# Two feed-forward blocks of a hybrid transformer: shared products in two alternating sets of four PSUM banks, and one weight sum moved to an accumulating transfer

## The chip, the cores and the metric

The kernel runs on one core of one Trainium2 chip. The metric is device time in microseconds (us) of one execution, as the median of the runs. A core has TensorE (PE, matmuls, with a sequencer for weight loads), VectorE (DVE), ScalarE (ACT), GpSimd (POOL), SyncE (SP, which here only issues transfers) and 16 DMA engines between HBM and the on-chip memory SBUF. Matmuls write to PSUM, used here as eight banks of 128 x 512 float32 values.

## The reference

Two layers over 256 tokens of width 2048, in float32. Each adds a mixer (gated delta rule and a linear recurrence in the first layer, two kinds of attention in the second) and then a feed-forward block of inner width 5632; a last norm follows.

```python
def swiglu(hn, w_gate, w_up, w_down):
    return (jax.nn.silu(hn @ w_gate) * (hn @ w_up)) @ w_down

for layer in range(DEPTH):
    h = h + mixer(rmsnorm(h, ...), ...)
    h = h + swiglu(rmsnorm(h, ffn_norm[layer]), ffn_w_gate[layer], ffn_w_up[layer], ffn_w_down[layer])
return rmsnorm(h, final_norm)
```

The change touches the two feed-forward blocks alone.

## The kernel before, in words

**Precision.** Every float32 operand is split into a high half (rounded to the matmul's type, by a cast on ScalarE) and a low half (the rest, by a subtraction on VectorE). A product is the sum of three matmuls: high by high, high by low, low by high. `X` and `hid` hold the split activations, 128 x 128 pieces of which are the stationary operand; the weights stream past as 128 x 512.

**Blocks.** `ffn` (from line 659) goes through 17 blocks per layer: 11 gate/up blocks of 512 inner columns and 6 down blocks, in three pieces of (4 gate/up + 2 down), (4 + 2), (3 + 2). A block has four output banks `F[t, i]`: token half `t` by column half `i` (gate or up; or the two 512-wide halves of the outputs). The weights of a block come as tiles of 128 x 1024 float32 (512 KB), one per step.

**Plain steps and sevens.** A plain step is one weight tile against both token halves: 12 matmuls. A "seven" takes a 2 x 2 arrangement of four weight tiles (b11, b12, b21, b22) and 2 x 2 activation blocks, and forms their product from seven products instead of eight, with sums of weight tiles and sums of activation tiles (`comb`, made by `combine`). A seven is seven steps of 6 matmuls. Most gate/up blocks have two sevens and 8 plain steps; the first block of a layer has none; the last down blocks have one.

Before, `steps` gives each block four banks `F` in the PSUM pool `acc` and four banks `M` for the shared products in the pool `msp`. At the block's end `ends` (from line 427) copies M0 out on ScalarE and makes the three sums on VectorE into a tile `e` of SBUF; `values` adds them to `F` (L721), applies scale and SiLU on ScalarE (L722) and multiplies gate and up (L727); `residual` adds `h` and `F` (L741, L746). `turned` transposes the result on TensorE (`Ph`, L673) and splits it into `hid`. The three weight sums of a seven are made on VectorE in a tile `T` (L485, L492), a fourth by an accumulating transfer from GpSimd's queue (L487).

**Order.** `stream` walks the list of steps and readies them four ahead: `load` (SP's queue, L175), the cast (L547), the low half (L560). From the second block of a layer on, TensorE, VectorE and ScalarE run in the order written; in the first block a scheduler orders them.

**Memory.** The pools `wr` (three raw tiles), `wh` and `wl` (high and low halves) live through the whole program. The pools `og`/`hid`, `fp` and `mx` are closed and opened anew for every mixer and every feed-forward stage (`phase`). `load` sets its count to -12 at a phase's start, so that the first twelve raw tiles of a stage come from `wr`; after that four of seven come from four buffers `raw4` in `mx`. High halves of two steps in six (`thi`) and low halves of two in five (`tlo`) lie in `fp`.

**The seam.** A stage is entered behind the mixer's output projection, whose last group `g` = 3 ends with the sums into `h` (L361), the squares of `h` for the norm (`sumsq`, L319, into a scratch tile `junk`), the transposes `Pt` (L328) and the split into `X` (L329, L330).

Of the kernel before, what the change touches and what calls it, by code (L numbers as in the profile page):

```python
# [11 lines left out]
T = 256  # L12
# [35 lines left out]
def body(tc, A, out):  # L48
# [266 lines left out]
    def sumsq(g, *ts):  # L315
        for t in ts or range(2):
            j = (mx.tile([128, 1024], F32, name="junk", tag="T", bufs=2)[:, 0:512] if more else
                 mx.tile([128, 512], F32, name="junk", tag="t2", bufs=4))
            S.activation(j, h[:, t, g * 512:(g + 1) * 512], AF.Square, accum_out=ssp[:, t, g:g + 1])  # L319
# [69 lines left out]
    def combine(f, r=None):  # L389

        c = mx.tile([128, 4, 2, 128], F32, name="cc4", tag="T", bufs=2)
# [12 lines left out]
    def combine_x(x4, r=None):  # L404

        f = mx.tile([128, 4, T], F32, name="cf", tag="T", bufs=2)
        V.tensor_tensor(out=f, in0=x4[:, :, 0].bitcast(F32), in1=x4[:, :, 1].bitcast(F32), op=ALU.add)
        return run(combine([f[:, :, t * 128:(t + 1) * 128] for t in range(2)], r))
# [29 lines left out]
    class Step:  # L438


        def __init__(self, high, use, unit=None):
            self.high, self.use, self.unit = high, use, unit

    def steps(src, x, comb, nd, early, late):

        ns = len(comb)
        plain = [(i, u) for m in range(nd) if m not in comb for u in (2 * m, 2 * m + 1) for i in range(2)]
        n, F, M = len(plain) // 2, {}, {}

        def bank(t, i):  # L450
            if (t, i) not in F:
                F[t, i] = Bank(acc.tile([128, 512], F32, name=f"F{t}{i}", tag="acc"), n + (ns if t * i == 0 else 0))
            return F[t, i]

        def bank7(j):
            if j not in M:
                M[j] = Bank(ms([128, 512], f"M{j}"), ns)
            return M[j]

        def xs(k, t):  # L460
            return [x(k)[:, j, t * 128:(t + 1) * 128] for j in range(2)]

        def high(i, u, b, name):
            def f():
                b[name] = load(src(i, u))
                return b[name]
            return f

        def simple(i, u):
            b = {}  # L470

            def use(w, tt=(0, 1)):
                for t in tt:
                    bank(t, i).add(lambda kk: xs(2 * u + kk, t), w)
            return Step(high(i, u, b, "b"), use, (i, use))

        def seven(m):
            b = {}
            cx = lambda i: lambda kk: [comb[m]()[:, j, i, kk] for j in range(2)]
            q = lambda j, t: lambda kk: xs(4 * m + 2 * j + kk, t)  # L480

            def first():
                load_b12()
                b["t"] = mx.tile([128, 1024], F32, name="T", tag="T", bufs=2)
                V.tensor_tensor(out=b["t"], in0=b["b11"], in1=b["b12"], op=ALU.add)  # L485

                G.dma_start(b["b12"], src(1, 2 * m + 1), accum_op=ALU.add)  # L487
                return b["t"]

            def more_of(name):  # L490
                def f():
                    V.tensor_tensor(out=b["t"], in0=b["t"], in1=b[name], op=ALU.add)  # L492
                    return b["t"]
                return f

            load_b12 = high(1, 2 * m, b, "b12")
            return [Step(high(0, 2 * m, b, "b11"), lambda w: bank7(0).add(q(0, 0), w)),
                    Step(first, lambda w: bank7(1).add(cx(0), w)),
                    Step(high(1, 2 * m + 1, b, "b22"), lambda w: bank(0, 1).add(cx(3), w)),
                    Step(more_of("b22"), lambda w: bank7(2).add(cx(2), w)),  # L500
                    Step(high(0, 2 * m + 1, b, "b21"), lambda w: bank(0, 0).add(q(1, 0), w)),
                    Step(more_of("b21"), lambda w: bank(1, 0).add(q(1, 1), w)),
                    Step(lambda: b["b12"], lambda w: bank7(3).add(cx(1), w))]

        sevens = [y for m in comb for y in seven(m)]
        plain = [simple(*y) for y in plain]
        if not sevens:
            return plain, F, M
        mid = len(plain) - early - late
        order = plain[:early]  # L510
        for g in range(mid + 1):
            order += sevens[g * len(sevens) // (mid + 1):(g + 1) * len(sevens) // (mid + 1)]
            order += plain[early + g:early + g + 1] if g < mid else plain[early + mid:]
        return order, F, M
# [16 lines left out]
    def stream(acts, guard):  # L531
# [4 lines left out]
        ready = [y for y in acts if isinstance(y, Step)]  # L536
        at = [0, 0]
        g = None

        def ahead(n):  # L540

            while at[0] < min(n + 1, len(ready)):
                y, k = ready[at[0]], at[0]
                y.raw = y.high()
# [6 lines left out]
            while at[1] < min(n, len(ready)):  # L551
                low(at[1])

        def low(k):
            if k < at[1]:
                return
            y = ready[k]
            y.lo = (fp.tile([128, 1024], F32R, name="tlo", tag="tlo", bufs=2) if k % 5 in (1, 3) else
                    wl.tile([128, 1024], F32R, name="wlo"))
            V.tensor_sub(y.lo, y.raw, y.hi.bitcast(F32))  # L560
            at[1] = k + 1

        n = 0
        for y in acts:
            if isinstance(y, Step):
                if y is guard[0]:
                    g = tc.manual_schedule(engines={V.engine, S.engine, PE.engine})
                    g.__enter__()
                ahead(n + 1 + 3)
                y.use((y.hi, y.lo))  # L570
                if y.unit:
                    tick()
                n += 1
            else:
                y()
# [81 lines left out]
    def ffn(L, then, fin=None):  # L657

        gu, dn = A[f"gu{L}"], A[f"dn{L}"]
        cx, ch, acts, guard, left = {}, {}, [], [None], []  # L660
        todo = {}

        def turned(hid, j, want, soon):
# [3 lines left out]
            def first():  # L667
                a = todo.pop(j)
                o["P"] = []
                for t in range(2):  # L670
                    P = ms([128, 4, 128], "Ph")
                    for i in range(4):
                        PE.transpose(P[:, i], a[:, 2 * t, i * 128:(i + 1) * 128], tb["ident"])  # L673
# [3 lines left out]
                if want:  # L677

                    o["f"] = [a[:, 2 * t + 1].rearrange("p (k n) -> p k n", n=128) for t in range(2)]
# [15 lines left out]


            put = {2: first, 3: second}
            if want:
                put.update({8: part, 14: part, **({19: last} if soon else {})})
            return put, [last] if want and not soon else []  # L700

        def spread(order, put):

            for n, y in enumerate(order):
                acts.extend(put.get(n, []))
                acts.append(y)

        def values(hid, j, F, M, ns):

            o = {}  # L710
            rs = lambda t: nrm["rs"][:, t:t + 1]

            def bank_sums():
                o["a"] = ends(M) if ns else sums()

            def half(i):
                def f():
                    for t in range(2):
                        v = o["a"][:, 2 * t + i]
                        if ns:  # L720
                            V.tensor_tensor(out=v, in0=F[t, i].t, in1=v, op=ALU.add)  # L721
                        S.activation(v, v if ns else F[t, i].t, AF.Copy if i else AF.Silu, scale=rs(t))  # L722
                return f

            def product():
                a = o["a"]
                V.tensor_tensor(out=a[:, 0::2], in0=a[:, 1::2], in1=a[:, 0::2], op=ALU.mult)  # L727
                todo[j] = a

            return bank_sums, half(0), half(1), product  # L730

        def residual(p, F, M):

            o = {}

            def bank_sums():
                o["e"] = ends(M)
                left[:] = [o["e"]]
                for t in range(2):
                    et = o["e"][:, 2 * t:2 * t + 2].rearrange("p a n -> p (a n)")  # L740
                    V.tensor_tensor(out=et, in0=h[:, t, 1024 * p:1024 * (p + 1)], in1=et, op=ALU.add)  # L741

            def half(i):
                def f():
                    for t in range(2):
                        V.tensor_tensor(out=h[:, t, (2 * p + i) * 512:(2 * p + i + 1) * 512], in0=F[t, i].t,  # L746
                                        in1=o["e"][:, 2 * t + i], op=ALU.add)
                return f

            return bank_sums, half(0), half(1)  # L750

        b, late, turn, rest, next_rest = 0, None, None, [], []
# [811 lines left out]
```

## Time and profile before

| | |
|---|---|
| Median of 3 runs | 2218.5 us (2218.19 to 2218.76) |
| Span of the profiled execution | 2217.3 us |
| TensorE busy | 2200.4 us (99%) |
| VectorE busy | 1961.3 us (88%) |
| ScalarE busy | 1333.7 us (60%) |
| Feed-forward stages in the trace | about 430 to 1125 us, and 1518 to 2208 us |
| Loads of the feed-forward weights | 352 + 176 from SP, 40 + 20 accumulating from GpSimd, 512 KB each |

The span runs from the first to the last instruction in the trace. Busy time of an engine is the union of its instructions; a matmul is drawn to the end of its pipeline, so neighbouring matmuls overlap in the drawing. In the lists of instructions the columns are start, length, engine, line, operation, output<-inputs, shapes; what stands in brackets is the idle time before it and the instruction that ended it. Groups give busy time, mean of one in ns, and idle time before.

### The profile page before, as it was taken

The numbers are of one execution on the slowest core, as the hardware profiler recorded it, in microseconds if no ns is written. First come the engines' busy times: TensorE is split into PE (matmuls) and PEld (weight loads), VectorE is DVE, ScalarE is ACT, GpSimd is POOL, SyncE is SP. The second block draws the span as 40 slices with busy tenths as digits, with TensorE's granted clock in tenths as the row PEclk, the third lists the DMA queues.
The fourth block names the chain that finished last, engine by engine and source line by source line (L and its number), as shares of the span: only waits on it lengthen the run. The fifth ranks groups of instructions, "written<-read, shape, count | busy, mean of one in ns | idle before, by whom it ended". The sixth has DMA issues, their size and how long they took to land.

```text
span 2217.3 us, 30619 instructions
## 1 busy us (share of the span) xinstructions
PE 2200.4 (99%) x10960; PEld 1840.2 (83%) x10960; DVE 1961.3 (88%) x2664; ACT 1333.7 (60%) x1787; POOL 54.0 (2%) x66
## 2 busy tenths in 40 slices
PE   9999999999999999999999999999999999999998
PEld 8888888888888888888888888888888888888886
DVE  8899676679999999999996688857899999999998
ACT  6786664556655666466664554545666566655665
POOL 0000000000000000000000000000000000000000
PEclk9999999999999999999999999999999999999999
DMA  7545446667777778677664565556678777777784
GB/s 284 158 145 167 136 151 188 204 210 222 235 226 247 211 215 246 214 229 235 195 201 154 154 188 171 162 181 218 204 214 237 232 224 222 237 224 233 232 243 138
DMA packets 126569, 453.79 MB, mean 205 GB/s; under 512 B 14128, under 2 KB 15664, under 8 KB 126288
## 3 DMA queue, kind: packets, MB, share of 16 engines
q1 hardware_dynamic: 117488, 420.10, 58.2%
q0 software_dynamic: 8640, 31.46, 8.5%
q8 instruction: 86, 1.41, 0.3%
q14 instruction: 67, 0.55, 0.1%
q10 hardware_dynamic: 288, 0.27, 0.0%
HBM read 449.68 MB, written 2.10 MB: 204 GB/s over the span
## 4 chain that ended last, share of the span: by engine, by line
PE 88%; DVE 8%; issue 2%; DMA 1%; ACT 1%; DVEq 0%; ACTq 0%; POOLq 0%; SPq 0%
PE F L420 14%; PE F L419 14%; PE F L421 14%; PE Pw L201 11%; PE Pw L206 6%; PE M L421 5%; PE M L419 5%; PE M L420 5%; PE Px L305 3%; PE Px L307 3%; PE Px L306 3%; DVE wlo L560 1%; PE Ph L673 1%; DVE e L721 1%; DVE tlo L560 1%
## 5 line engine op out<-in xcount | busy, mean ns | idle before, releaser
L181 ACT CAST whi<-raw 128x1024 fp32r<-128x1024 f32 x245 | 256.8, 1051 | 261.7 <-PE Pw L201 85.3
L547 ACT CAST whi<-raw 128x1024 fp32r<-128x1024 f32 x362 | 372.0, 1048 | 51.1 <-PE F L421 31.1
L182 DVE TENSOR_TENSOR wlo<-raw,whi 128x1024 fp32r<-128x1024 f32 x245 | 299.0, 1222 | 114.7 <-PE Pw L206 37.2
L201 PE MATMUL Pw<-X,whi 128*128 128x512 f32 x1088 | 388.3, 400 | 0.0
L206 PE MATMUL Pw<-X,wlo 128*128 128x256 f32 x1088 | 304.6, 280 | 0.2
L419 PE MATMUL F<-whi,X 128*128 128x512 f32 x698 | 273.1, 391 | 0.6 <-DVE h L746 0.6
L421 PE MATMUL F<-whi,X 128*128 128x512 f32 x698 | 272.1, 390 | 0.0
L560 DVE TENSOR_TENSOR wlo<-raw,whi 128x1024 fp32r<-128x1024 f32 x214 | 260.6, 1220 | 9.2 <-ACT whi L547 5.3
L420 PE MATMUL F<-wlo,X 128*128 128x512 f32 x650 | 253.2, 390 | 0.0
L201 PEld LDWEIGHTS Pw<-X,whi 128*128 128x128 f32 x1088 | 204.2, 188 | 47.2 <-issue 0.5
L547 ACT CAST whi<-T 128x1024 fp32r<-128x1024 f32 x110 | 116.1, 1055 | 197.2 <-DVE T L492 119.1
L206 PEld LDWEIGHTS Pw<-X,wlo 128*128 128x128 f32 x1088 | 205.3, 189 | 1.6 <-DVE wlo L182 0.7
L560 DVE TENSOR_TENSOR tlo<-raw,whi 128x1024 fp32r<-128x1024 f32 x148 | 180.6, 1220 | 7.9 <-ACT whi L547 6.0
L547 ACT CAST thi<-raw 128x1024 fp32r<-128x1024 f32 x166 | 173.5, 1047 | 13.6 <-PE F L421 8.7
L419 PEld LDWEIGHTS F<-whi,X 128*128 128x128 f32 x698 | 131.1, 188 | 27.7 <-issue 1.1
L421 PEld LDWEIGHTS F<-whi,X 128*128 128x128 f32 x698 | 131.0, 188 | 27.3
L547 ACT CAST thi<-T 128x1024 fp32r<-128x1024 f32 x70 | 74.0, 1057 | 130.9 <-DVE T L485 61.9
L492 DVE TENSOR_TENSOR T<-T,raw 128x1024 f32<-128x1024 f32 x120 | 146.7, 1223 | 1.7
L420 PE MATMUL F<-tlo,X 128*128 128x512 f32 x370 | 144.1, 389 | 0.3 <-DVE tlo L379 0.3
L420 PEld LDWEIGHTS F<-wlo,X 128*128 128x128 f32 x650 | 122.1, 188 | 24.9
L560 DVE TENSOR_TENSOR wlo<-raw,thi 128x1024 fp32r<-128x1024 f32 x102 | 124.5, 1221 | 8.5 <-PE F L420 4.4
L419 PE MATMUL F<-whi,hid 128*128 128x512 f32 x336 | 131.3, 391 | 0.0
(445 smaller groups left out, 4691.1 us busy)
## 6 DMA issues: line engine op xcount, KB each, us to landing
raw<-in_gu SPq DMA_DIRECT2D x352, 512.0 KB, 4.6
raw<-in_dn SPq DMA_DIRECT2D x176, 512.0 KB, 4.7
raw<-in_w0w SPq DMA_DIRECT2D x72, 512.0 KB, 3.7
raw<-in_wo SPq DMA_DIRECT2D x64, 512.0 KB, 3.6
raw<-in_w1w SPq DMA_DIRECT2D x64, 512.0 KB, 3.6
raw<-in_gu POOLq DMA_DIRECT2D x40, 512.0 KB, 7.8
raw<-in_w1x SPq DMA_DIRECT2D x32, 512.0 KB, 3.7
raw<-in_dn POOLq DMA_DIRECT2D x20, 512.0 KB, 7.3
```

The lines of the kernel that those rows point to most:

```text
L181: S.copy(hi, raw)
L182: V.tensor_sub(lo, raw, hi.bitcast(F32))
L201: PE.matmul(P.rearrange("p a b -> p (a b)"), hi[:, kk], X[:, k].rearrange("p a b -> p (a b)"), start=k == 0, stop=False)
L206: PE.matmul(P[:, 0], lo[:, kk], X[:, k, 0], start=False, stop=k == NK - 1)
L305: PE.matmul(Ps[t], x[:, 0, ts], hi[:, kk], start=k == 0, stop=False)
L306: PE.matmul(Ps[t], x[:, 0, ts], lo[:, kk], start=False, stop=False)
L419: PE.matmul(self.t, xh, hi[:, kk], start=self.i == kk == 0, stop=False)
L420: PE.matmul(self.t, xh, lo[:, kk], start=False, stop=False)
L421: PE.matmul(self.t, xl, hi[:, kk], start=False, stop=kk == 1 and self.i == self.n - 1)
L492: V.tensor_tensor(out=b["t"], in0=b["t"], in1=b[name], op=ALU.add)
L547: S.copy(y.hi, y.raw)
L560: V.tensor_sub(y.lo, y.raw, y.hi.bitcast(F32))
```

## The change

- A class `Mix` takes the place of `steps`, `Bank` and the `M` banks. The shared products go into the block's own four banks: M0 into F00, the second into F01, the third into F11, the fourth into F10. Between steps `middle` turns these into the output sums, in PSUM: a copy of F00 to SBUF (ScalarE), two sums (VectorE), a copy back to F01 (ScalarE), two more sums (VectorE). Then the remaining products of the sevens and the plain steps are added on top.
- Blocks use the pools `acc` and `msp` in turn. The last four plain steps of a block are placed between the first products of the next.
- `values` and `residual` read the banks directly.
- Of the three weight sums of a seven, two stay on VectorE, in place in the tile of b11; the third (adding b21) is a second accumulating transfer from GpSimd.
- Raw tiles have tags: `ha`, `hb`, `hc` (two buffers each in `mx`) for b11, b12, b22, and `raw` for the others, five buffers of which three are in `wr` and two in `mx`. Loads are asked for up to eight steps ahead. In the first block of a layer the first ten steps take turns over `raw`, `ha`, `raw`, `hb`, `raw`, `hc`.
- Scratch tiles `T` and `e` go; `a` and `de` (one buffer each) come. `hid` is one tile for the whole stage. GpSimd's descriptor area in SBUF is set to 8192 bytes.

```diff
-            j = (mx.tile([128, 1024], F32, name="junk", tag="T", bufs=2)[:, 0:512] if more else
+            j = (mx.tile([128, 1024], F32, name="junk", tag="a", bufs=1)[:, 0:512] if more else
...
+    class Mix:
...
+            sevens = [self.seven(m) for m in comb]
+            self.early = [y[i] for i in range(4) for y in sevens]
+            self.direct = [y[i] for i in range(4, 7) for y in sevens]
...
+        def simple(self, i, u, first):
...
+            k = 2 * u + i
+            return Step(("raw", "ha", "raw", "hb", "raw", "hc")[k % 6] if first and k < 10 else "raw",
+                        lambda raw: nc.sync.dma_start(raw, self.src(i, u)), use, unit=(i, use))
...
+            def first_sum():
+                V.tensor_tensor(out=b["b11"], in0=b["b11"], in1=b["b12"], op=ALU.add)
                 G.dma_start(b["b12"], src(1, 2 * m + 1), accum_op=ALU.add)
...
+            def second_sum():
+                V.tensor_tensor(out=b["b11"], in0=b["b11"], in1=b["b22"], op=ALU.add)
+                return b["b11"]
+
+            def third_sum():
+                G.dma_start(b["b11"], src(0, 2 * m + 1), accum_op=ALU.add)
+
+            y = [Step("ha", get("b11", 0, 2 * m), lambda w: self.add(0, 0, q(0, 0), w)),
+                 Step("hb", get("b12", 1, 2 * m), lambda w: self.add(0, 1, cx(0), w), first_sum),
+                 Step("hc", get("b22", 1, 2 * m + 1), lambda w: self.add(1, 1, cx(2), w), second_sum, third_sum),
+                 Step(None, None, lambda w: self.add(1, 0, cx(1), w), lambda: b["b12"]),
+                 Step(None, None, lambda w: self.add(0, 1, cx(3), w), lambda: b["b22"]),
+                 Step("raw", get("b21", 0, 2 * m + 1), lambda w: self.add(0, 0, q(1, 0), w)),
+                 Step(None, None, lambda w: self.add(1, 0, q(1, 1), w), lambda: b["b11"])]
...
+        def middle(self):
...
+            def copy():
+                o["d"] = mx.tile([128, 2, 512], F32, name="de", tag="de", bufs=1)
+                S.copy(o["d"][:, 0], F[0, 0])
+
+            def sums():
+                d, e = (o["d"][:, j] for j in range(2))
+                V.tensor_tensor(out=d, in0=F[1, 1], in1=d, op=ALU.add)
+                V.tensor_tensor(out=e, in0=F[0, 1], in1=d, op=ALU.subtract)
+
+            def back():
+                S.copy(F[0, 1], o["d"][:, 1])
+
+            def last():
+                d, e = (o["d"][:, j] for j in range(2))
+                V.tensor_tensor(out=F[1, 1], in0=e, in1=F[1, 0], op=ALU.subtract)
+                V.tensor_tensor(out=F[1, 0], in0=F[1, 0], in1=d, op=ALU.add)
+
+            n = self.ns
+            return [(self.early[n - 1], 1, copy), (self.early[3 * n - 1], 1, sums), (self.early[3 * n - 1], 2, back),
+                    (self.early[4 * n - 1], 1, last)]
...
+        def loads_to(n, must=False):
+            while at[2] < min(n, len(order)):
+                y = order[at[2]]
+                if y.tag:
+                    q = slots.setdefault(y.tag, [])
+                    if len(q) == (5 if y.tag == "raw" else 2):
...
+                    q.append(y.free)
+                    if y.tag == "raw":
+                        count_raw[0] += 1
+                    y.raw = (wr.tile([128, 1024], F32, name="raw") if y.tag == "raw" and count_raw[0] % 5 in (0, 2, 4) else
+                             mx.tile([128, 1024], F32, name=y.tag, tag=y.tag, bufs=2))
+                    y.load(y.raw)
+                at[2] += 1
...
+            loads_to(n + 8)
+            ahead(n + 1 + 3)
+            y.use((y.hi, y.lo))
...
+            def gate():
+                o["a"] = mx.tile([128, 2, 512], F32, name="a", tag="a", bufs=1)
+                for t in range(2):
+                    S.activation(o["a"][:, t], Y.F[t, 0], AF.Silu, scale=rs(t))
+
+            def product():
+                for t in range(2):
+                    v = o["a"][:, t]
+                    V.scalar_tensor_tensor(out=v, in0=Y.F[t, 1], scalar=rs(t), in1=v, op0=ALU.mult, op1=ALU.mult)
...
+                space = (msp, "ms") if len(blocks) % 2 else (acc, "acc")
...
+        order, tail = [], []
+        for Y in blocks:
+            e = list(Y.early)
+            r = -(-len(e) // len(tail)) if tail else 0
+            while e or tail:
+                order += e[:r] + tail[:1]
+                e, tail = e[r:], tail[1:]
+            cut = len(Y.plain) - 4 * (Y is not blocks[-1])
+            d, body, tail = list(Y.direct), Y.plain[:cut], Y.plain[cut:]
+            Y.first = (d + body + tail)[0]
+            while d or body:
+                order += d[:2] + body[:1]
+                d, body = d[2:], body[1:]
+            events += (Y.middle() if Y.ns else []) + Y.after
...
-    nc = _bacc.Bacc("TRN2", target_bir_lowering=False, num_devices=1)
+    nc = _bacc.Bacc("TRN2", target_bir_lowering=False, num_devices=1, dynamic_dma_scratch_size=8192)
```

More of the change, by code (lines that the diff above doesn't have):

```diff
@@ L389, in combine @@
     def combine(f, r=None):
-        c = mx.tile([128, 4, 2, 128], F32, name="cc4", tag="T", bufs=2)
+        c = mx.tile([128, 4, 2, 128], F32, name="cc4", **(dict(tag="a", bufs=1) if more else dict(tag="T", bufs=2)))
         if r is None:
@@ L438, in body, with __init__ @@
     class Step:
[L441 to L469, printed above, removed]
+        def __init__(self, tag, load, use, ready=None, after=None, unit=None):
+            self.tag, self.load, self.use, self.ready, self.after, self.unit = tag, load, use, ready, after, unit
+            self.needs, self.free = [], self
@@ L505, in steps @@
[L505 to L514, printed above, removed]
+                    self.add(t, i, lambda kk: self.xs(2 * u + kk, t), w)
@@ L694, in last, with values, residual @@
                 ch[j] = run(o["c"])
[L697 to L710, printed above, removed]
-            rs = lambda t: nrm["rs"][:, t:t + 1]
-            def bank_sums():
-                o["a"] = ends(M) if ns else sums()
+            return o, [(3, first), (4, second)] + ([(6, part), (8, part), (9, last)] if want else [])
+        def values(Y, hid, j, want):
+            rs = lambda t: nrm["rs"][:, t:t + 1]
+            o, later = turned(Y, hid, j, want)
+            def gate():
[6 more added lines that the diff above has]
+                    V.scalar_tensor_tensor(out=v, in0=Y.F[t, 1], scalar=rs(t), in1=v, op0=ALU.mult, op1=ALU.mult)
+            return [(Y.plain[-1], 0, gate), (Y.plain[-1], 1, product)] + [(Y.plain[-1], *z) for z in later]
+        def residual(Y, p):
             def half(i):
@@ L730, in values @@
[L730 to L750, printed above, removed]
@@ L752, in ffn @@
-        b, late, turn, rest, next_rest = 0, None, None, [], []
+                        hs = h[:, t, (2 * p + i) * 512:(2 * p + i + 1) * 512]
+                        V.tensor_tensor(out=hs, in0=Y.F[t, i], in1=hs, op=ALU.add)
+                return f
+            return [(Y.plain[-1], 0, half(0)), (Y.plain[-1], 1, half(1))]
+        hid = ogp.tile([128, 16, 2, T], F32R, name="hid", tag="hid")
+        b, events = 0, []
         for groups, down in (((0, 2, 2, 2), (2, 2)), ((2, 2, 2, 2), (2, 2)), ((2, 2, 2), (1, 1))):
@@ L779, in ffn @@
+                space = (msp, "ms") if len(blocks) % 2 else (acc, "acc")
+                if j < piece:
+                    Y = Mix(lambda i, u, b=b: gu[b, u, i], lambda k: X[:, k], {m: lambda m=m: cx[m] for m in range(groups[j])}, 4,
+                            *space, first=b == 0)
+                    Y.after = values(Y, hid, j, j < max(down))
                     b += 1
@@ L808, in ffn @@
+        stream(order, puts, blocks[1].early[0])
         if not fin:
```

228 lines of the change are left out of this document (115 added, 113 removed).

## The prediction, made before the changed kernel ran

> **What bounds the kernel now.** I read the page's busy times, then the two feed-forward stages by windows, then TensorE's stops in them, then the seams at which a feed-forward stage begins.
>
> ```profile
> span 2217.3 us, 30619 instructions
> ...
> PE 2200.4 (99%) x10960; PEld 1840.2 (83%) x10960; DVE 1961.3 (88%) x2664; ACT 1333.7 (60%) x1787; POOL 54.0 (2%) x66
> ...
> q0 software_dynamic: 8640, 31.46, 8.5%
> ```
>
> The span is 2217.3 us and the median of the runs 2218.5: 1.2 us lie around the span, and I carry them over. Windows over the two stages:
>
> ```profile
> 430.00:1125.00 695.00, 692.61 (x3104) 572.06 (x3104) 661.00 (x665) 422.20 (x482) 26.04 (x30) 1.00 0.74 223
> 1518.00:2208.00 690.00, 688.75 (x3083) 569.74 (x3082) 657.05 (x661) 419.52 (x479) 25.89 (x30) 1.00 0.74 222
> ```
>
> TensorE (third number) is idle for 2.39 and 1.25 us, 3.64 us in 1385, at a granted clock of 1.00. VectorE is busy for 661.00 and 657.05, close behind. Is a busy TensorE at its pace? Its timeline at the end of one block and at the boundary between a down block and the next gate block:
>
> ```profile
> 563.69 0.39 PE L421 MATMUL F<-thi,X 128*128 128x512 f32 x1
> 563.91 0.39 PE L419 MATMUL F<-thi,X 128*128 128x512 f32 x1
> ...
> 564.37 0.39 PE L421 MATMUL F<-thi,X 128*128 128x512 f32 x1
> 565.00 1.09 PE L673 MATMUL Ph<-tab,e 128*128 128x128 f32 x8 [0.24 <-DVE e L727]
> ...
> 933.13 0.39 PE L421 MATMUL F<-whi,hid 128*128 128x512 f32 x1
> 934.07 0.47 PE L419 MATMUL F<-whi,X 128*128 128x512 f32 x1 [0.56 <-DVE h L746]
> ```
>
> Starts stand 0.227 us apart (563.69 to 564.37 is three steps), though each matmul is drawn 0.39 long. So 0.16 us of every stop hides under the drawn end: at 564.37 the next start is 0.63 away, 0.40 more than the pace, and 0.24 of it is shown as idle. A product step (6 matmuls) is 1.36 us, a plain step (12) 2.72.
>
> ```profile
> PEld Ph L673 <- DVE e L727: 6.0, 8, 0.9
> ...
> L673 PE MATMUL Ph<-tab,e 128*128 128x128 f32 x176 | 23.2, 275 | 2.7 <-DVE e L727 2.7
> ```
>
> So eight times in two stages TensorE waits for VectorE's product of gate and up values: 2.7 idle + 8 x 0.16 = 4.0 us. With the stop at 933.13 (0.56 + 0.16 = 0.7) that is **4.7 us, all that this change can win inside the stages**. VectorE is nearly full, but that costs almost nothing yet.
>
> **The change part by part.** *Products.* A seven stays seven steps of 6 matmuls, a plain step 12, a block's turning 8 transposes: no matmul goes or comes, at an unchanged pace: 0.
>
> *VectorE's sums.*
>
> ```profile
> L492 DVE TENSOR_TENSOR T<-T,raw 128x1024 f32<-128x1024 f32 x120 | 146.7, 1223 | 1.7
> L434 DVE TENSOR_TENSOR e<-M,e 128x1024 f32<-128x1024 f32 x34 | 41.6, 1224 | 1.1
> L721 DVE TENSOR_TENSOR e<-F,e 128x512 f32<-128x512 f32 x80 | 52.3, 686 | 3.2 <-PE F L421 3.0
> L727 DVE TENSOR_TENSOR e<-e 128x1024 f32<-128x1024 f32 x22 | 26.9, 1223 | 4.8 <-ACT e L722 4.8
> ```
>
> One weight sum in three leaves VectorE: 60 x 1.22 = 73 us. Adding `e` to `F` (52.3) goes; the product (26.9) becomes two 512-wide operations, 2 x 0.69 on 22 blocks = 30. Turning the bank sums in place (four of 512 for two of 512 and one of 1024) comes out even. With the residual's lighter form VectorE has some 125 to 150 us less in 1318. The worth is the stops it caused, 4.0 of the 4.7 us. No row has VectorE or ScalarE writing sums into PSUM. The nearest, 512-wide reads from PSUM, take 0.69; the 1024-wide ones 1.22. I take 0.69, with 0.6 and 1.3 as ends. They hide: from the last `cx2` product to the first product on the turned `F01` lie two plain and two product steps, 8.2 us, against two VectorE operations and a ScalarE copy, about 2.1 us (3.9 at the upper end). The sum into `F10` is due one plain and two product steps, 5.4 us, after the last `cx1` product and takes 1.4 to 2.6. Queued behind them on VectorE are later low halves; four prepared steps cover those. Without that cover it would be 2 us a block, on 32 blocks with sevens: 64 us.
>
> *Two sets of banks.* Gate, product and residual now read one pool while TensorE fills the other, and the transposes come three steps (5.4 us) after the block's last matmul instead of two. Needed before them: two gates on ScalarE, a product on VectorE, about 2.5 us by the rows. So the eight stops and the one at 933 go: -4.7 (0 to -4.7).
>
> *The last weight sum by a transfer*: 60 more accumulating transfers on POOL's queue.
>
> ```profile
> L487 POOL DMA_DIRECT2D raw<-in_gu x40: 862/862/1005, 467.7 to 2122.1; - x40
> ...
> DMA to landing us min/median/max: 5.8/7.5/10.8
> ```
>
> It is issued after the low half of the second sum and is due 7 product and 4 plain steps later, 20 us, against a landing of 7.5 (10.8 at most): hidden. POOL's next instruction in order is the next seven's accumulation, with a whole block to spare. The old accumulation is now due 10.9 us of products after its issue, plus the lead of some four steps: hidden as well. Load: 60 such transfers took 8.5% of the engines' span (188 us of 2217), so the stages go from a DMA share of 0.74 to 0.74 + 188/1385 = 0.88. Loads, looked up eight steps ahead, become later, not late: each buffer comes free seven or more steps before the next use. With the share under 1 I charge nothing; what it costs if that is wrong is the collision rival below. [...]
>
> *Where the first weights lie.* This decides my forecast. Before, the first twelve weight tiles of a feed-forward stage go to `wr`, the pool that outlives the phases, and are fetched while the mixer still runs. After, `loads_to` gives `wr` to every `raw` tile whose count modulo 5 is 0, 2 or 4; the count is raised first, so the very first (step 0) is number 1 and goes to `mx`, and step 1 has the tag `ha`, also in `mx`. `mx` is opened anew for the stage. When may a tile of it be written?
>
> ```profile
> 417.06 12.12 SPq L175 DMA_DIRECT2D raw<-in_gu  x5
> ...
> 430.29 0.39 PE L419 MATMUL F<-whi,X 128*128 128x512 f32 x1
> 431.97 0.40 PE L419 MATMUL F<-whi,X 128*128 128x512 f32 x1
> ...
> 431.75 0.19 ACT L319 ACTIVATION_READ_ACCUMULATOR junk<-h 128x1 f32 x1
> 433.27 2.01 ACT L547 CAST thi<-raw 128x1024 fp32r<-128x1024 f32 x2
> ...
> 431.97 1.23 DVE L407 TENSOR_TENSOR cf<-X 128x1024 f32<-128x1024 f32 x1 [0.79 <-ACT junk L319]
> ...
> 431.96 0.33 SPq L175 DMA_DIRECT2D raw<-in_gu  x1
> ```
>
> Today's first loads go out from 417.06, 13 us before the first feed-forward matmul at 430.29. But `cf`, the first tile of the new phase's `mx`, waits for `junk`, the old phase's last, and starts at 431.97, when the read of `junk` ends (431.75 + 0.19). The first load into the phase's own tiles goes out at 431.96, and `thi`, in another new pool, is first written after that. The second seam shows the same:
>
> ```profile
> 1519.02 0.19 ACT L319 ACTIVATION_READ_ACCUMULATOR junk<-h 128x1 f32 x1
> ...
> 1519.23 0.33 SPq L175 DMA_DIRECT2D raw<-in_gu  x1
> ...
> 1519.24 1.23 DVE L407 TENSOR_TENSOR cf<-X 128x1024 f32<-128x1024 f32 x1 [0.79 <-ACT junk L319]
> ```
>
> So the load of step 0 cannot start before 431.96 and 1519.23. Steps 0 and 1 open all four banks, so steps already in `wr` cannot go first. From there:
>
> ```profile
> raw<-in_gu SPq DMA_DIRECT2D x2, 512.0 KB, 5.0
> ...
> raw<-in_gu SPq DMA_DIRECT2D x2, 512.0 KB, 4.2
> ...
> raw<-in_wo SPq DMA_DIRECT2D x64, 512.0 KB, 3.6
> ...
> 1513.50 1.05 ACT L547 CAST whi<-raw 128x1024 fp32r<-128x1024 f32 x1 [0.29 <-DMA raw<-in_gu]
> ...
> 1514.86 1.22 DVE L560 TENSOR_TENSOR wlo<-raw,whi 128x1024 fp32r<-128x1024 f32 x1 [0.82 <-ACT whi L547]
> ```
>
> Landing: 5.0 and 4.2 are medians of two loads issued together at the two seams; a mixer load takes 3.6. The first of a burst is near the latter: 3.7. Cast 1.05. VectorE starts 0.31 after the cast's end and takes 1.22; hand-overs add 0.15. That is 431.96 + 6.43 = 438.4 for the first low half. By then TensorE has done the transposes and two high-half matmuls; before, it had done three at 431.97. Lost: 438.4 - 431.97 + 0.23 = 6.7 us, and at the second seam the same from 1519.23. Sum **+13.3** (bounds 10 with an early landing and high halves first, 17 with a landing of 5.0 and step 1 late too). TensorE runs at its pace for the rest of the stage, so nothing gives it back. It was covered by the early load; the change removes that cover.
>
> *The rest.* Tiles `cf`, `cc4`, `junk` and `f` move to single buffers `de` and `a`, whose uses follow each other on one engine or lie whole steps apart: 0. The final row of adds loses the sums before it, but the last add still follows the last matmul: 0 (-1 to 0). The smaller descriptor area in SBUF only makes room: 0.
>
> Sum: 2217.3 + 13.3 - 4.7 = 2225.9 span, 2227.1 with the 1.2 around it. Its own range is 2224 (+10 - 4.7) to 2235 (+17 - 0).
>
> **The rivals.** *The seam costs nothing* (not slower): a tile of the new `mx` waits only for an old tile at its own addresses. If step 0's buffer lay where nothing was in use late, its load would go out as early as today, from about 417. For it: no row names the addresses. Against it: three different first writers (SP, VectorE, ScalarE) start together behind `junk` at both seams. It decides when the first load precedes the first feed-forward matmul by more than about 6.4 us. Time: 2218.5 - 4.7 = 2213.8.
>
> *Transfers collide.* With a share of 0.88, the accumulations, 7.5 us now, come after their 10.9 us plus lead; ScalarE's next cast waits, and TensorE some 0.5 us in each of 32 blocks: +16 on the forecast, 2243. For it: 10.8 at the slowest now. Against: four prepared steps.
>
> *Half a seam*: high halves and transposes fill more of the wait, or step 0 lands sooner, so that 3 to 4 us are lost at each seam: about 2220.
>
> **How the numbers follow.** Forecast 0.66, no seam 0.16, collision 0.11, half a seam 0.07. About 0.2% (4.4 us: 2214.1 to 2222.9) is what a measurement can tell from no change. Half a seam lies inside it, and half of no seam (a gain not quite full): same 0.15. Faster 0.08, slower 0.66 + 0.11 = 0.77. From 2219 to 2237 the forecast, half a seam and the milder collisions are held; no seam is left out.
>
> **What would show it.** At both seams, TensorE idle for 5 us or more before the first feed-forward matmul, put down to the cast of step 0 or its load, and that load issued right after the last `junk`. Ph's wait for VectorE gone from the groups. VectorE below 1200 us over the two stages, TensorE's pace still 0.227. Twice the packets on q0, DMA share near 0.88. Wrong would be a first load issued some 13 us before the seam, or stops of TensorE inside the blocks.

## The result and the profile after

The changed kernel takes 2230.0 us (2229.5 to 2230.7), against 2218.6 us (2218.2 to 2219.6) for the kernel before, measured beside it: a ratio of 1.0052, 95% interval [1.0037, 1.0066]. It is slower, by about 11.4 us. One run of eleven of a later version, the one with the first three chunks in the open buffers, took 4494.6 us and is left out of its ratio. The lines of the changed kernel's page that answer those shown of before:

```profile
span 2227.5 us, 30574 instructions
...
PE 2203.5 (99%) x10960; PEld 1844.0 (83%) x10960; DVE 1829.3 (82%) x2554; ACT 1341.4 (60%) x1775; POOL 106.2 (5%) x126
...
q1 hardware_dynamic: 117488, 420.10, 54.6%
q0 software_dynamic: 17280, 62.92, 16.4%
...
L473 PE MATMUL F<-whi,X 128*128 128x512 f32 x712 | 279.2, 393 | 9.9 <-ACT whi L608 9.9
```

The span is 10.2 us longer, though VectorE is busy for 132 us less. The last line names the place: 9.9 us in which TensorE has nothing to do ahead of a product with a new high half. Windows over the two feed-forward stages (the third number is TensorE's busy time, the seventh VectorE's; then ScalarE, GpSimd, the granted clock, the DMA share, GB/s):

```profile
428.00:1130.00 702.00, 696.53 (x3120) 576.33 (x3119) 598.26 (x613) 430.47 (x482) 52.08 (x60) 1.00 0.81 245
1520.00:2218.50 698.50, 693.13 (x3094) 573.35 (x3092) 594.78 (x613) 428.38 (x478) 51.97 (x60) 1.00 0.81 243
```

VectorE has 1193 us of work there, 125 less than before, and TensorE is idle for more, not less: 5.5 and 5.4 us. Where, the timeline of the first seam shows (start, length, engine, line, operation, output<-inputs; in brackets the idle time ahead of it):

```profile
430.43 0.39 PE L307 MATMUL Px<-whi,Od 128*128 128x512 f32 x1
430.92 1.33 PE L328 MATMUL Pt<-tab,h 128*128 128x128 f32 x8
...
432.18 0.19 ACT L319 ACTIVATION_READ_ACCUMULATOR junk<-h 128x1 f32 x1
...
432.39 0.33 SPq L488 DMA_DIRECT2D raw<-in_gu  x1
432.40 1.23 DVE L407 TENSOR_TENSOR cf<-X 128x1024 f32<-128x1024 f32 x1 [0.85 <-ACT junk L319]
...
436.03 1.99 ACT L608 CAST whi<-raw 128x1024 fp32r<-128x1024 f32 x2 [2.21 <-DMA raw<-in_gu]
437.11 2.36 DVE L620 TENSOR_TENSOR wlo<-raw,whi 128x1024 fp32r<-128x1024 f32 x2 [0.38 <-ACT whi L608]
437.12 1.22 PE L473 MATMUL F<-whi,X 128*128 128x512 f32 x2 [4.87 <-ACT whi L608]
438.38 0.79 PE L474 MATMUL F<-wlo,X 128*128 128x512 f32 x1
438.98 0.63 PE L475 MATMUL F<-whi,X 128*128 128x512 f32 x1
439.40 0.63 PE L473 MATMUL F<-whi,X 128*128 128x512 f32 x1
...
443.49 0.39 PE L474 MATMUL F<-tlo,X 128*128 128x512 f32 x1
```

The load of step 0 goes out when the last read of `junk` has ended (432.18 + 0.19), lands, is cast, and the first low half is used at 438.38. Then the matmuls do not run at their pace of 0.227 us: from 438.38 to 440.68 their starts stand 0.42 to 0.60 us apart. A few short windows over the two seams:

```profile
434.50:440.50 6.00, 3.33 (x7) 2.23 (x8) 5.62 (x11) 4.47 (x5) 0.00 (x0) 0.50 1.01 399
...
1528.60:1533.00 4.40, 4.26 (x9) 2.96 (x10) 4.32 (x4) 4.40 (x6) 0.00 (x0) 0.50 1.01 408
```

The granted clock is 0.50 there. In the trace's records of the clock it is halved from 433.99 to 440.82 and from 1526.26 to 1533.09, 6.83 us each time; before, it stays full until 2211.50, behind the last matmul (2207.80, 0.39 long). The second seam:

```profile
1521.83 0.39 PE L307 MATMUL Px<-whi,Om 128*128 128x512 f32 x1
...
1528.70 1.22 PE L473 MATMUL F<-whi,X 128*128 128x512 f32 x2 [5.05 <-ACT whi L608]
1529.96 0.79 PE L474 MATMUL F<-wlo,X 128*128 128x512 f32 x1
...
1535.38 0.39 PE L474 MATMUL F<-tlo,X 128*128 128x512 f32 x1
```

And the timeline of the kernel before, for the price of a seam:

```profile
430.06 0.39 PE L307 MATMUL Px<-whi,Od 128*128 128x512 f32 x1
...
435.64 0.40 PE L421 MATMUL F<-whi,X 128*128 128x512 f32 x1
...
1517.33 0.39 PE L307 MATMUL Px<-whi,Om 128*128 128x512 f32 x1
...
1522.92 0.40 PE L421 MATMUL F<-whi,X 128*128 128x512 f32 x1
```

I take a seam as the time from the start of the mixer's last matmul to the start of the twentieth of the stage, the last line of each pair: 5.58 and 5.59 us before, 13.06 and 13.56 after. So the seams cost 7.5 and 8.0 us, **15.5 us together**. The rest of the two stages, from the twentieth matmul to the last one, became **5.7 us shorter**; the mixers and the tail after the last matmul add some 0.5. That is the 10.2 us.

The tile `Ph`, before and after, with what its engines waited for (us, times; TensorE and its weight loads are both counted):

```profile
L673 PE MATMUL Ph<-tab,e x176: 272/273/329, 480.3 to 2150.8; 128*128 128x128 f32 x176
...
  DVE e L727: 8.7, 16
```

```profile
L735 PE MATMUL Ph<-tab,a x176: 270/272/273, 499.0 to 2166.4; 128*128 128x128 f32 x176
```

After, no row puts a wait of the transposes down to VectorE; the longest transpose takes 273 ns where it took 329.

### The profile page after: what moved, and what is told of

It reads as the page before. It is cut to its first block, busy times and chain, and to the rows that moved or that the text cites. A ratio compares the mean times of both kernels' runs of the same rounds, so it can differ in the third digit from the quotient of the medians.

```text
span 2227.5 us, 30574 instructions
## 1 busy us (share of the span) xinstructions
PE 2203.5 (99%) x10960; PEld 1844.0 (83%) x10960; DVE 1829.3 (82%) x2554; ACT 1341.4 (60%) x1775; POOL 106.2 (5%) x126
## 3 DMA queue, kind: packets, MB, share of 16 engines
q1 hardware_dynamic: 117488, 420.10, 54.6%
q0 software_dynamic: 17280, 62.92, 16.4%
## 4 chain that ended last, share of the span: by engine, by line
PE 97%; DVE 1%; DMA 1%; ACT 0%; issue 0%; DVEq 0%; ACTq 0%; SPq 0%
PE F L474 20%; PE F L473 20%; PE F L475 20%; PE Pw L201 11%; PE Pw L206 6%; PE Px L305 3%; PE Px L306 3%; PE Px L307 3%; PE F L420 1%; PE F L421 1%; PE Ph L735 1%; PE F L419 1%; PE Psc L1365 1%; PE Pw L247 0%; PE Pt L328 0%; PE Pw L248 0%
## 5 line engine op out<-in xcount | busy, mean ns | idle before, releaser
L181 ACT CAST whi<-raw 128x1024 fp32r<-128x1024 f32 x245 | 256.8, 1051 | 266.3 <-PE Pw L201 86.4
L182 DVE TENSOR_TENSOR wlo<-raw,whi 128x1024 fp32r<-128x1024 f32 x245 | 298.8, 1220 | 118.7 <-PE Px L306 37.7
L608 ACT CAST whi<-raw 128x1024 fp32r<-128x1024 f32 x238 | 249.4, 1054 | 109.9 <-PE F L475 88.1
L608 ACT CAST whi<-ha 128x1024 fp32r<-128x1024 f32 x152 | 160.5, 1056 | 167.0 <-DVE ha L503 41.4
L474 PE MATMUL F<-wlo,X 128*128 128x512 f32 x588 | 230.4, 392 | 0.1
L620 DVE TENSOR_TENSOR wlo<-raw,whi 128x1024 fp32r<-128x1024 f32 x140 | 170.3, 1219 | 4.6 <-ACT whi L608 0.9
L474 PE MATMUL F<-tlo,X 128*128 128x512 f32 x420 | 163.4, 389 | 0.0
L620 DVE TENSOR_TENSOR wlo<-ha,whi 128x1024 fp32r<-128x1024 f32 x96 | 117.4, 1222 | 37.4 <-ACT whi L608 25.6
L608 ACT CAST thi<-ha 128x1024 fp32r<-128x1024 f32 x92 | 97.3, 1057 | 76.4 <-DVE ha L503 32.6
L473 PE MATMUL F<-whi,hid 128*128 128x512 f32 x336 | 131.2, 390 | 0.0
L475 PE MATMUL F<-whi,hid 128*128 128x512 f32 x336 | 130.8, 389 | 0.0
L608 ACT CAST thi<-raw 128x1024 fp32r<-128x1024 f32 x100 | 105.2, 1052 | 36.7 <-PE F L475 32.1
L474 PE MATMUL F<-wlo,hid 128*128 128x512 f32 x320 | 124.5, 389 | 0.0
```

What stands on the lines that cost most here:

```text
L181: S.copy(hi, raw)
L182: V.tensor_sub(lo, raw, hi.bitcast(F32))
L473: PE.matmul(P, xh, hi[:, kk], start=z[0] == 1 and kk == 0, stop=False, skip_group_check=skip)
L474: PE.matmul(P, xh, lo[:, kk], start=False, stop=False, skip_group_check=skip)
L475: PE.matmul(P, xl, hi[:, kk], start=False, stop=kk == 1 and z[0] in z[1:], skip_group_check=skip)
L608: S.copy(y.hi, y.raw)
```

## The experiments

### Step 0 in the buffers that stay open

```diff
-  y.tag == "raw" and count_raw[0] % 5 in (0, 2, 4)
+  y.tag == "raw" and count_raw[0] % 5 in (1, 2, 4)
```

> The changed kernel, with one number other: raw tiles number 1, 2 and 4 of five lie in the lasting pool instead of 2, 4 and 5, so that step 0 of a feed-forward stage has its tile there, and step 1 (tag ha) still in the pool that opens with the stage. Theory (the seam: TensorE waits for the load of the first tile, which waits for the mixer's last use of its pool): the load of step 0 goes out some 13 us before the seam, steps 0 and 2 (24 matmuls, 5.4 us) fill most of the wait for step 1, and of the 6.9 and 7.6 us lost at the two seams 0 to 2 us each are left: 2217 to 2220 us. Rival (the cost sits in the blocks themselves: collisions of transfers, or the new waits on sums in PSUM): no more than 1 us comes back, 2229 to 2230. Rival (the first tile waits only at its own addresses, something else is late): no change, 2230.

Measured: 2216.3 us, ratio 0.9990 [0.9981, 0.9999], a little under what was expected. One number in one condition takes 13.7 us off the changed kernel. From the mixer's last matmul to the twentieth it is 5.54 us at both seams, as before, and the clock stays full (0.999 over the span, as before; 0.996 in the changed kernel). What is left is step 1, whose tile `ha` still lies in the reopened pool. The timeline of this kernel:

```profile
436.88 1.05 ACT L608 CAST thi<-ha 128x1024 fp32r<-128x1024 f32 x1 [2.39 <-DMA ha<-in_gu]
...
437.98 0.72 PE L473 MATMUL F<-thi,X 128*128 128x512 f32 x2 [0.22 <-ACT thi L608]
...
439.24 0.50 PE L474 MATMUL F<-tlo,X 128*128 128x512 f32 x1 [0.30 <-DVE tlo L620]
```

ScalarE waits for the load of `ha`, and TensorE for the two halves: about 1 us of stops at each seam.

### The first three chunks there

```diff
-  ("raw", "ha", "raw", "hb", "raw", "hc")[k % 6]     # first ten steps of a stage
+  ("raw", "raw", "raw", "ha", "hb", "hc")[k % 6]
...
-  count_raw[0] % 5 in (0, 2, 4)
+  count_raw[0] % 5 in (1, 2, 3)
```

> The changed kernel with steps 0, 1 and 2 of a stage in the lasting pool (the tags of the first ten steps start raw, raw, raw, ha, hb, hc, and raw tiles number 1, 2 and 3 of five lie there). Theory (seam): TensorE goes on without a stop at both seams as in the kernel before, and what the banks in turn take away inside the stages (4.7 us of stops) is left as a gain: 2213 to 2216 us, faster than before (2218.6). Rival (cost in the blocks): 2229 to 2230.

Measured: 2214.7 us, ratio 0.9982 [0.9973, 0.9991]. The timeline of this kernel:

```profile
417.43 12.12 SPq L488 DMA_DIRECT2D raw<-in_gu  x5
...
430.44 0.39 PE L307 MATMUL Px<-whi,Od 128*128 128x512 f32 x1
430.67 0.39 PE L473 MATMUL F<-whi,X 128*128 128x512 f32 x1
...
432.34 0.33 SPq L488 DMA_DIRECT2D ha<-in_gu  x1
```

The first loads go out 13 us ahead, the stage starts 0.23 us behind the mixer, and only `ha`, `hb` and `hc`, in the reopened pool, still wait: the first of them goes out at 432.34. The seam is the whole loss of the change; without it, all that the change does is worth some 4 us of gain.

### The kernel before, with its first loads late

```diff
-  loads[0], extra[0] = -12, 0
+  loads[0], extra[0] = -12 if mixer else 0, 0
```

> The kernel before, with one number other: the count of raw tiles starts at 0 instead of -12 in a feed-forward stage, so that its first and third tile come from the four buffers of the pool that opens with the stage. Nothing else of the change is in it. Theory (seam): the same wait appears in the old kernel, load of step 0 issued right behind the last junk, TensorE idle for about 5 us at each seam and slow for some 3 us after it, 6 to 8 us each: 2230 to 2235 us. Rival (the wait needs the new blocks, tags or deeper look-ahead): within 1 us of before, 2218 to 2220.

Measured: 2236.1 us, ratio 1.0078 [1.0064, 1.0091], above what was expected. The timeline at its first seam:

```profile
434.00 10.32 SPq L175 DMA_DIRECT2D raw<-in_gu  x9
...
438.68 1.22 PE L419 MATMUL F<-whi,X 128*128 128x512 f32 x2 [4.81 <-ACT whi L547]
```

The seams, measured as above, are 13.40 and 13.76 us long, 7.8 and 8.2 more than before. The mean granted clock is 0.996, as in the changed kernel, and from 439.70 to 443.54 the starts stand 0.42 to 0.43 us apart: the same wait without any other part of the change. The 2 us beyond that lie ahead of the first seam: the mixer's last matmul starts at 432.04 instead of 430.06. In the other profiles this start lies between 430.43 and 431.71 (431.05 and 431.18 in two more versions of the kernel before), and the profiled execution was the longest of the four: at least half of the 2 us is how much the first mixer varies from execution to execution. Whether the edit adds the rest is open.

### Filling the wait, to hold the clock

Matmuls of 256 columns whose results nothing uses are put between the mixer and the first step of the changed kernel. Three versions: 44 on `X[:, 12]`, 48 and then 34 on `X[:, 8]`.

```diff
+  Pz = ms([128, 512], "Pfill")
+  for _ in range(44):
+      PE.matmul(Pz[:, 0:256], X[:, 0, 0, 0:128], X[:, 12, 0], start=True, stop=True)
```

> The changed kernel with 44 idle-filling matmuls of 256 columns (results not used) on TensorE in the wait at each seam, behind the transposes. Theory (TensorE's clock falls while it idles for 5 us, and the nine matmuls after the wait are slow for that reason alone): they run 0.227 us apart again, 2 us come back per seam, 2225 to 2227 us, the wait itself unchanged. Rival (the slow matmuls wait for operands or are slowed by the burst of loads): they stay 0.43 to 0.67 us apart, 2230 us or more.

> The changed kernel with 48 filling matmuls of 256 columns (results not used) in the wait at each seam, on an operand that is there early, so that they start right behind the transposes and end near 438 us, where the low half of step 0 is ready. In e4 the filling started 2.1 us late and overran that point by 2.9 us. Theory (TensorE's clock falls while it idles): filling and first feed-forward matmuls run at full pace, and 1.5 to 2.2 us come back per seam, 2225 to 2227.5 us. Rival (operands or the burst of loads slow the first matmuls): 0.43 us and more apart as in the changed kernel, 2229 to 2231.

> The changed kernel with 34 filling matmuls in each seam's wait instead of 48 (their results are used by nothing), so that they end at about 438.2 us, when the first low half is there. Theory (about 2 us of each seam are the half clock that follows the idle wait): the clock stays at full speed, the matmuls of the first step start at about 438.2 and at full pace, the tenth at about 440.3 instead of 441.2, some 0.9 us less per seam against the changed kernel: about 2228.2 us. Rival (the pace there is set by the loads and casts that run beside it, not by the clock): no gain, 2230 us.

Measured: 2231.5 us, ratio 1.0058 [1.0044, 1.0071]; 2231.8 us, 1.0061 [1.0046, 1.0077]; 2230.3 us, 1.0047 [1.0034, 1.0061]. None won the time that was expected. The timeline of the second, with 48:

```profile
434.12 6.00 PE L792 MATMUL Pfill<-X 128*128 128x256 f32 x48 [1.81 <-DVE X L330]
439.96 0.40 PE L473 MATMUL F<-whi,X 128*128 128x512 f32 x1
440.19 0.40 PE L474 MATMUL F<-wlo,X 128*128 128x512 f32 x1
```

The fillers themselves wait for `X`, start some 2 us late, and end at 439.96, after the low half is there. But the pace is what was asked about: at a granted clock of 1.00 from 428 to 443, the very first matmuls stand 0.23 us apart, while from 439 to 443 the DMA share is 1.02, VectorE is busy for 4.00 of the 4.00 us and ScalarE for 3.40. The changed kernel has 1.01 and both engines busy throughout from 437.1 to 441, where its starts are slow. So the slow starts are the clock, not the loads and casts beside them. The version with 34 shows the clock at work (windows of its first seam):

```profile
434.00:435.00 1.00, 0.66 (x5) 0.66 (x6) 1.00 (x4) 0.09 (x1) 0.00 (x0) 1.00 0.50 193
435.00:436.00 1.00, 1.00 (x7) 1.00 (x6) 1.00 (x4) 0.00 (x0) 0.00 (x0) 0.57 0.91 356
```

After a wait of 1.81 us (as the matmuls are drawn; 2.05 by the weight loads) the clock was halved from about 435.1 to 438.6, with the fillers already running since 434.34. They took longer for it, 5.82 us for 34 where 48 took 6.00, so the first step began at 440.00 again and nothing was won. That a wait filled from its first moment would save the 1.3 to 1.6 us per seam is argued, not shown.

### The third weight sum back on VectorE

The version with three chunks in the open buffers, but `b11 += b21` done by VectorE. These are the central lines; the step that uses the sum now also waits for the load of `b21`:

```diff
-  G.dma_start(b["b11"], src(0, 2 * m + 1), accum_op=ALU.add)
+  V.tensor_tensor(out=b["b11"], in0=b["b11"], in1=b["b21"], op=ALU.add)
```

> e2_three_in_wr with the third weight sum of a seven back on VectorE (an addition of the loaded b21 in place of the second accumulating transfer). VectorE gets 73 us back, the added transfers go. Theory (two sets of banks alone take the eight stops away, VectorE having slack, and the transfers cost nothing): the same as e2 within 1 us, 2214 to 2215.5. Rival (the relief of VectorE by the transfer is what took the stops away): the stops at the transposes come back in part, 2216 to 2219. Rival (the added transfers cost hidden time): faster than e2, below 2213.5.

Measured: 2214.1 us, ratio 0.9979 [0.9970, 0.9987]; with the transfer it was 0.9982 [0.9973, 0.9991]. Windows of this kernel:

```profile
428.00:1125.00 697.00, 696.44 (x3129) 576.55 (x3128) 628.63 (x645) 426.48 (x485) 26.04 (x30) 1.00 0.71 224
1516.00:2204.00 688.00, 688.00 (x3084) 570.34 (x3083) 620.52 (x639) 421.06 (x476) 25.91 (x30) 1.00 0.71 223
```

VectorE works 59 us more than with the transfers, the DMA share falls to 0.71, and TensorE stops neither here nor there. Sixty transfers neither cost nor win anything that can be measured.

### What made TensorE stop at the transposes before

The kernel before, with its third weight sum left out (so its results lack it):

```diff
-  Step(more_of("b21"), lambda w: bank(1, 0).add(q(1, 1), w)),
+  Step(lambda: b["t"], lambda w: bank(1, 0).add(q(1, 1), w)),
```

> The kernel before, leaving out the third weight sum of each seven (the last product takes the sum of two tiles in place of three, so the outputs are not the reference's). VectorE loses the same 73 us as by the change, the banks stay as they were. Theory (the stops come from the row of bank sums, scale and product behind a block's last matmul in one set of banks): most of the eight stops stay, 2216.5 to 2218.5 us. Rival (they come from VectorE being nearly full): they go, 2214 to 2216.

Measured: 2214.0 us, ratio 0.9977 [0.9968, 0.9986]. All eight stops are gone, with one set of banks and the old row of sums at the block's end: no row puts a wait of `Ph` down to VectorE, and its longest transpose takes 273 ns, as after the change.

```profile
L673 PE MATMUL Ph<-tab,e x176: 272/272/273, 481.3 to 2146.0; 128*128 128x128 f32 x176
```

My theory, that this row makes the stops whatever else VectorE does, fell. The next run put idle work in the sum's place: three additions of 256 columns into a tile that nobody reads, the third sum still left out.

```diff
+  z = mx.tile([128, 256], F32, name="Z", tag="Z", bufs=1)
+  for _ in range(3):
+      V.tensor_tensor(out=z, in0=b["t"][:, 0:256], in1=b["b21"][:, 0:256], op=ALU.add)
```

> The kernel before with its third weight sum left out (its time then was 2214.0 us), but with three additions of 256 columns into a small tile that nobody reads put where the sum stood, so that VectorE works about as long as before (three times some 0.42 us for the 1.22 of the sum) and nothing depends on it. The third weight sum stays left out of the result. Theory (the stops of TensorE come from the time that VectorE is held at that place): the stops at the transposes of h come back, and the time is 2217.5 to 2219.2 us, as before. Rival (they come from the chain of results: the low half of the sum waits for the sum, the sum for its load): no stops, 2213.5 to 2215 us.

Measured: 2218.0 us, ratio 0.9996 [0.9987, 1.0005]: the gain is all but gone again. Its tile `Ph`:

```profile
L679 PE MATMUL Ph<-tab,e x176: 271/273/329, 481.4 to 2150.4; 128*128 128x128 f32 x176
...
  DVE e L733: 8.1, 16
```

The waits of `Ph` are back (8.1 us in 16 entries, 8.7 before). Nothing depends on the idle additions, so it is the time for which VectorE is held, and not the chain from load to sum to low half, that stops TensorE there.

### How much room the two sets of banks leave

Two loads on VectorE, each some 73 to 76 us by the durations (60 x 1.22 and 180 x 0.42), put into the 2214.1 us version (two sets, no seam wait, third sum on VectorE). First, each first-tile subtraction of a seven done twice; then the three idle additions ahead of each third sum.

```diff
-  V.tensor_sub(y.lo, y.raw, y.hi.bitcast(F32))
+  for _ in range(2 if y.tag == "ha" and not y.unit else 1):
+      V.tensor_sub(y.lo, y.raw, y.hi.bitcast(F32))
```

> The version with the first three chunks of the stage's blocks in the tags reserved from the start (no wait at the seam, two sets of banks, the third weight sum on VectorE; 2214.1 us), with one step of each block done twice on VectorE: the subtraction that makes a low half is repeated with the same operands, 60 times 1.22 us, about 73 us more of VectorE over the two stages, so that its busy time comes back to about 1320 us, as in the kernel before. Theory (VectorE's load is what makes TensorE stop at the transposes of h, whatever set the banks are in): the stops come back in some blocks and the time is 2216 to 2219 us. Rival (two sets of banks alone take the stops away): no stops and 2214 to 2215.5 us.

```diff
             def third_sum():
+                z = mx.tile([128, 256], F32, name="Z", tag="Z", bufs=1)
+                for _ in range(3):
+                    V.tensor_tensor(out=z, in0=b["b11"][:, 0:256], in1=b["b12"][:, 0:256], op=ALU.add)
```

> The version with no wait at the seam, two sets of banks and the third weight sum on VectorE (2214.1 us), with three additions of 256 columns into a small tile that nobody reads ahead of each third sum: some 73 us more on VectorE over the two stages, as much as in the run that repeated the subtraction (2248.0 us), but in another place and with nothing depending on it directly. Theory (VectorE has no 73 us to spare in these stages, wherever they lie): TensorE stops at low halves again, 2222 to 2248 us. Rival (the repeated subtraction cost so much because it lay ahead of low halves that were just due): 2214 to 2217 us.

Measured: 2248.0 us, ratio 1.0132 [1.0118, 1.0146], and 2273.7 us, 1.0248 [1.0234, 1.0262]. Both are far above either expectation: VectorE's busy time rises from 1889.3 us to 1952.3 and 1958.3, by 63 and 69; of that, 34 and 60 appear in the time. The stops are not at the transposes; the groups of the second kernel put them at products that wait for a low half:

```profile
L474 PE MATMUL F<-wlo,X 128*128 128x512 f32 x588 | 232.8, 396 | 12.1 <-DVE wlo L624 11.6
L474 PE MATMUL F<-tlo,X 128*128 128x512 f32 x420 | 166.8, 397 | 10.6 <-DVE tlo L624 9.6
```

One window over the start of a block, the same stretch of time without the load and then with it, shows how full VectorE is there:

```profile
549.00:575.00 26.00, 26.00 (x116) 21.56 (x115) 25.56 (x26) 17.45 (x19) 0.90 (x2) 1.00 0.76 224
```

```profile
549.00:575.00 26.00, 24.93 (x109) 19.97 (x109) 25.86 (x26) 18.45 (x21) 1.73 (x2) 1.00 0.63 168
```

VectorE is already busy for 25.56 of 26.00 us without the load, where a block's sums and low halves come close together; over the whole stage it is at 0.90. The idle additions do not lie in this window but just ahead of it, and TensorE's stop comes inside it (timeline of the kernel with them):

```profile
535.78 1.34 DVE L514 TENSOR_TENSOR Z<-ha,hb 128x256 f32<-128x256 f32 x3
...
553.38 0.50 PE L474 MATMUL F<-tlo,X 128*128 128x512 f32 x1 [0.99 <-DVE tlo L624]
```

VectorE comes late to the start of the block (the second sum of `b11` and `b12` starts at 553.24 instead of 548.70), has no room to catch up in this stretch, and TensorE pays. In these two versions, then, two sets of banks do not free the kernel from VectorE: the tight place moves from the transposes to the start of the block. With about as much VectorE work as the kernel before (1952.3 and 1958.3 us against 1961.3) they are even 29 and 55 us slower than it, so where that work lies counts for more than its sum. The transfers in the changed kernel give VectorE slack that nothing there needs yet.

## Why the prediction was right, and where it was off

Forecast 2227.1 us, measured 2230.0, slower as forecast and for the reason given.

- *The seam decides.* Right. The load of step 0 was to leave with the last `junk`: it did (432.39), and `cf` with it. The trace also has loads that left well ahead of the seam, at 417.42, 420.25 and 422.88, which the prediction names as a sign against it; they are those of steps 2, 6 and 8, whose tiles lie in the open buffers, and do not let step 0 start sooner. The first low half, forecast at 438.4, was used at 438.38. That the two agree so closely is luck: the load left 0.43 us later than forecast (432.39, not 431.96; the mixer's last matmul started 0.37 later), and the way from it to the low half took 5.99 us instead of 6.43. With step 0 in the open buffers the loss is gone; the kernel before with late loads has the same seams. Of the waits for a whole closed pool the runs show the effect: tiles of the reopened pool wait, those of the open one don't. In the built program step 0's tile at the second seam (bytes 186560 to 190656 of a partition) doesn't overlap `junk` (203584 to 211776), and the mixer had made its last low half of a weight tile by 1514.3, while the load left at 1523.79. So it is the pool it waits for, and the rival of own addresses falls. One of the three witnesses for this in the prediction is none: ScalarE's `thi` at 433.27 comes right behind ScalarE's own work on `X` (431.85, 1.55 long).
- *"TensorE runs at its pace for the rest of the stage": this step failed.* The term of 6.7 us per seam was mis-sized. From the first low half to the twentieth matmul are 17 steps, 3.86 us at the pace of 0.227. They took 5.11 us (438.38 to 443.49) and 5.42 us (1529.96 to 1535.38): 1.25 and 1.56 us are the halved clock, for which the prediction had no term. The wait itself cost 7.48 - 1.25 = 6.2 and 7.97 - 1.56 = 6.4 us, a little under the 6.7.
- *The gain inside the stages.* Forecast 4.7 us, found 5.7 between the twentieth and the last matmul. By the starts in the two traces 3.9 of it lie just ahead of the first transposes, 0.5 among the transposes, 0.8 at stops between products like the one at 933.13; the rest is spread too thin to place. The prediction laid it to two sets of banks and to VectorE's lighter load together. The first isn't needed: taking one sum per seven from VectorE removes the stops with the old banks.
- *VectorE.* 125 us less in the stages, the lower end of the 125 to 150; sums written into PSUM took 0.69 us, as assumed, and cost TensorE no stop.
- *The transfer is hidden.* Right, and the rival in which transfers collide falls: with the transfers and without, the time is the same. The DMA share is 0.81, not near 0.88. GpSimd's transfers do take time of the same 16 engines (q0's 16.4%), but a share of 0.81 left room enough. The term for q0 held (8.5% to 16.4% of the span, 177 us), but the plain loads took less of the engines for the same 420.10 MB, 54.6% instead of 58.2% of the span, some 74 us. With the third sum back on VectorE the loads and transfers are those of before, and the DMA share of the stages is 0.71 instead of 0.74, so the added transfers are not the whole of it; why, no run tells.
- *Around the span.* 1.2 us were carried over; it was 2230.0 - 2227.5 = 2.5. So 1.3 of the 2.9 us by which the time exceeds the forecast lie outside the span, and 1.6 inside: the seams 15.5 for 13.3, the gain 5.7 for 4.7, and 0.5 in mixers and tail. Both differences set a median of several runs against the span of one; execution by execution it is about 1.8 us for the kernel before and 2.0 to 2.2 after, so most of the 1.3 is scatter.
- *The other rivals.* "The seam costs nothing" was forecast at 2213.8; the version built to have no seam wait takes 2214.7 and, with the sum on VectorE, 2214.1. "Half a seam" did not occur.

The two versions with three chunks in the open buffers, with and without the transfer, beat both kernels: 0.18% and 0.21% under the kernel before, 4 to 5 us.

## What to carry to other kernels

When a change moves buffers, look first at what is loaded ahead of the next phase and whether its tile lies in a pool that is open by then: the wait behind the closed pool cost 7.5 to 8.0 us per phase here, and moving the first tile alone out of it gave 13.7 us back over two phases. A busy share over a stage hides the stretch that is full (VectorE's 0.90 here, with 25.56 of 26.00 us at a block's start); look at windows as long as one block before giving an engine more work. And before crediting a new structure with a gain, take only the load off the old one: here that gave the same gain, some 5 us.

## What was unexpected of the hardware

A wait of TensorE cost more than its length here. After an idle 4.87 us (5.05 at the second seam) the granted clock was 0.50 for 6.83 us, a stretch that began within the wait (433.99, the wait ending at 437.12), and behind the first low half the matmuls started 0.41 to 0.60 us apart instead of 0.227 until it was full again. In the three versions with fillers the gap ahead of them at the first seam was the same: 1.81 us behind the drawn end of the transposes, 3.6 us from the start of the mixer's last matmul. By the windows the clock was halved for some 3.4 us at both seams in two of them (44 and 34 fillers) and not at all in the third (48), so the length of the gap alone did not decide. What did, no run here tells.
